# Normalised tokens stored as they are, the residual's gain and bias applied where the tokens return, in a two-layer diffusion backbone

## The chip, the cores and the metric

The kernel runs on one core of a Trainium2 chip. The time is device time of one execution in microseconds (us). Engines are called by the profile's names: PE is TensorE (PEld its weight loads), DVE VectorE, ACT ScalarE, POOL GpSimd, SP the engine on whose queue the kernel issues its DMAs. Each engine works through its own instructions in order.

## The reference

1024 latent tokens and 256 context tokens of width 1024, all fp32, pass two layers. Both layers end in a SwiGLU network of hidden width 2816. Layer 0 mixes with a gated convolution and a spatial gating unit, layer 1 with attention (8 heads, 2 key/value heads) over all tokens; the output is the latents'.

```python
def _post_norm(x, y, gate, g, b):
    return _layernorm(ALPHA * x + gate * y, g, b)

for l in range(DEPTH):
    m_lat = jnp.split((s_lat @ ada_w[l] + ada_b[l])[:, None, :], 6, axis=-1)
    m_ctx = jnp.split(s_ctx @ ada_w[l] + ada_b[l], 6, axis=-1)
    ...   # y_lat, y_ctx: convolution and gating unit (l = 0), or attention (l = 1)
    x = _post_norm(x, y_lat, m_lat[2], ln_g[l, 0], ln_b[l, 0])
    x = _post_norm(x, _swiglu(_modulate(x, m_lat[3], m_lat[4]), ffn_w_in[l], ffn_w_out[l]),
                   m_lat[5], ln_g[l, 1], ln_b[l, 1])
    ...   # the same for ctx in layer 0
```

So each normalised token is used twice: modulated, as input of the next product, and times ALPHA, as the residual of the next norm. With n the normalised token before gain and bias, the residual is n * (ALPHA * ln_g) + ALPHA * ln_b.

## The kernel before

The code is written against a tile framework whose scheduler orders the instructions of all engines by a simulated time line, within the dependences and the rings of buffers; it may move an instruction far ahead of or behind its place in the code. Rings are named by the tile: U (`u`), T (`tt`) and M2 (`m2`, shown as `m`) are general 128x512 buffers, T with few of them, and a weight pool has rings `raw`, `sw`, `w2`. An fp32 product is three products of split values (high x high, high x low, low x high; `mm3`, L88 to L90); `split` (L199 ACT copy, L200 DVE subtraction) makes the halves.

The order of work is: mixer for latents, then for context (0 to about 500 us); `ffn_in2` and `ffn_out2` for layer 0's latents (500 to 1185); the context's network, called from a hook in the last group of `ffn_out2` (to 1450); q, k, v (to 1600); attention (to 1905); the product with wo (to 2000); `ffn_in2` (2060 to 2450) and `ffn_out2` (to 2685) of layer 1; the last norm.

`ffn_in2` computes a pair of input products in seven products instead of eight: `ln_forms` transposes and modulates the normalised tokens to H and F (L483 to L493), `t_forms` makes four differences of them (L497) and splits them, and `weights(j)` makes seven weight forms for each of 22 column tiles. A tile uses the products in the order 1, 2, 6, 5, 7, 3, 4, where 6, 5, 7 and 4 take the forms t2, t1, t3 and t4. The first two products of the first `pre` tiles are made early. `ffn_out2` works in two halves of the hidden width (`kb`), for two halves of the columns (`h`) and two groups of four token tiles; DVE adds the residual `xr` to a sum (L646).

`ln_norm` normalises a tile: statistics on DVE, rs = (variance)^-0.5 on POOL (L212), the subtraction and product on DVE (L220). `resid` (L236 product, L239 sum, rows from `ln_row`, scaled on POOL at L227) then turns the normalised tile into the residual in place, 32 DVE steps for the latents' 16 half tiles, and `spill` stores it in DRAM. It is called after both latent mixers between `ln_forms` and `t_forms`; after `ffn_out2` of layer 0 it waits in `deferred`, which the context's network runs later.

`bg_ada` is a generator that makes the modulation vectors in the background: `step(n)` runs n of its pieces. A piece loads two blocks of ada_w and adds them up on DVE (L126, one step a block and vector); after four pieces POOL sums over partitions (`partition_all_reduce`, L132). (1, 1) and (1, 5) below are the layer and the index of such a vector.

Of the kernel before, what the change touches and what calls it, by code (L numbers as in the profile page):

```python
# [28 lines left out]
def hybrid_kernel(ctx: ExitStack, tc: tile.TileContext, A, out):  # L29
# [193 lines left out]
    def ln_row(nm, l, i, h, scale=True):  # L223
        t = M2([P, 512])
# [285 lines left out]
    def ffn_in2(pp, wq, l, H, act_d, steps=0, pre=2):  # L510
        def weights(j):
# [55 lines left out]
        for j in range(pre):  # L567
            p2(ready[j])
# [30 lines left out]
    def ffn_out2(pp, wq, l, act_d, xr, acc, steps=0, hook=None):  # L599
# [3 lines left out]
        for kb in range(2):  # L603
            aT = []
            for h in range(2):
                ws = []
                for k in range(KB):
# [13 lines left out]
                    hi = wq.tile([P, 512], F32R, tag="w2", name="w2", bufs=26)  # L621
                    lo = wq.tile([P, 512], F32R, tag="w2", name="w2", bufs=26)
                    split(w, hi, lo)
                    ws.append((hi, lo))
                for gi, grp in enumerate(grps):
# [3 lines left out]
                    pss = {}  # L629
# [8 lines left out]
                    def evict(t):  # L638
                        if kb == 0:
                            if h == 0:  # L640
                                acc[t] = [U([P, 512], F32), U([P, 512], F32)]
                            x = M2([P, 512])
                            nc.sync.dma_start(out=x, in_=xr[t * P:(t + 1) * P, h * 512:(h + 1) * 512])
# [9 lines left out]
                    else:  # L653
# [5 lines left out]
                        if kb == 1:  # L659
                            step(steps)  # L660

    def spill(xr):
        return lambda tiles, t0: (lambda t, h: nc.sync.dma_start(
            out=xr[(t0 + t) * P:(t0 + t + 1) * P, h * 512:(h + 1) * 512], in_=tiles[t][h]))
# [107 lines left out]
    for i in range(4):  # L772
        t_forms(H, F, i)
# [9 lines left out]
    def ctx_ffn_start():  # L783
# [8 lines left out]
        resid([accc[0], accc[1]], 0, 0, [nc.vector])  # L792
# [18 lines left out]
    xr_d = dp.tile([SEQ, D], F32, name="xr_d")  # L811
    hT = []
    for g in range(2):
        for t in range(4 * g, 4 * g + 4):
            ln_norm(acc[t])
        hT.append(ln_mod(pp, [acc[t] for t in range(4 * g, 4 * g + 4)], so))
    accl2 = [acc[t] for t in range(8)]
    deferred.append(lambda: resid(accl2, 0, 1, ENG, lambda t, h: nc.sync.dma_start(
        out=xr_d[t * P:(t + 1) * P, h * 512:(h + 1) * 512], in_=accl2[t][h])))
# [347 lines left out]
```

## Time and profile before

| | us |
|---|---|
| median of 3 runs | 2713.39 (2711.13 to 2713.71) |
| the profiled execution | 2716.35 |
| its span in the trace | 2714.6 |
| PE busy | 2548.0 (94%) |
| DVE busy | 1893.7 (70%) |
| ACT busy | 923.8 (34%) |
| POOL busy | 393.3 (14%) |
| mean granted PE clock | 0.972 of full speed |

Shares are of the whole span. What an engine does in a stretch, and what PE waits for there, is read from windows and from the idle time that the timeline gives in brackets before an instruction, with the engine and the instruction that ended it.

### The profile page before, as it was taken

How to read it: one execution, taken by the hardware profiler on the slowest of the kernel's cores; microseconds unless marked ns; L12 is line 12 of the kernel's file. 1: busy time of each engine (PE TensorE's matmuls, PEld its weight loads, DVE VectorE, ACT ScalarE, POOL GpSimd, SP SyncE). 2: the span in 40 equal slices, each digit the busy share in tenths (PEclk: the TensorE clock that was granted, in tenths of full speed). 3: DMA queues.
4: the chain of work that ended last, by engine and by line, in shares of the span. 5: the costliest groups of instructions: out<-in, count | busy, mean ns of one | idle time of the engine just before them, and what ended most of it. 6: DMA issues, size and time to landing. Idle time of an engine off the chain costs nothing. (4 is left out here: it accounts for less than half of the span.)

```text
span 2714.6 us, 34771 instructions
## 1 busy us (share of the span) xinstructions
PE 2548.0 (94%) x12956; PEld 2142.1 (79%) x12956; DVE 1893.7 (70%) x3203; ACT 923.8 (34%) x1628; POOL 393.3 (14%) x277
## 2 busy tenths in 40 slices
PE   8999986899999999967999999999978999999998
PEld 6778875787788887856997879999856888888886
DVE  3888497999966726767776767777599666665355
ACT  2311142433233412125443347777134333332121
POOL 0232031022200001230002432222030000000004
PEclk9999997999999999978999999999998999999999
DMA  7462144344422625535552200000412222235231
GB/s 248 137 199 86 57 132 161 132 152 137 124 92 72 221 78 184 182 118 171 187 177 95 106 13 1 25 24 24 147 55 105 93 72 91 77 120 181 85 105 62
DMA packets 152650, 307.39 MB, mean 113 GB/s; under 512 B 25312, under 2 KB 44768, under 8 KB 152480
## 3 DMA queue, kind: packets, MB, share of 16 engines
q1 hardware_dynamic: 152480, 305.16, 34.1%
q8 instruction: 102, 1.67, 0.2%
q14 instruction: 68, 0.56, 0.1%
HBM read 259.95 MB, written 45.15 MB: 112 GB/s over the span
## 5 line engine op out<-in xcount | busy, mean ns | idle before, releaser
L88 PE MATMUL mm<-u,w 128*128 128x512 f32 x1232 | 481.6, 393 | 30.5 <-ACT u L199 12.8
L90 PE MATMUL mm<-u,w 128*128 128x512 f32 x1232 | 476.1, 391 | 9.6 <-DVE w L200 9.6
L89 PE MATMUL mm<-u,w 128*128 128x512 f32 x1232 | 481.8, 391 | 1.7 <-DVE u L490 1.7
L199 ACT CAST w<-sw 128x512 fp32r<-128x512 f32 x264 | 163.1, 622 | 535.6 <-PE mm L89 397.4
L88 PEld LDWEIGHTS mm<-u,w 128*128 128x128 f32 x1232 | 232.6, 189 | 84.3 <-ACT u L199 13.7
L88 PE MATMUL mm<-w,u 128*128 128x512 f32 x704 | 275.1, 391 | 6.7 <-DVE u L646 4.6
L90 PEld LDWEIGHTS mm<-u,w 128*128 128x128 f32 x1232 | 232.5, 189 | 59.5 <-DVE w L200 11.0
L200 DVE TENSOR_TENSOR w<-sw,w 128x512 fp32r<-128x512 f32 x264 | 191.2, 727 | 125.8 <-ACT w L199 79.3
L89 PE MATMUL mm<-w,u 128*128 128x512 f32 x704 | 275.1, 391 | 0.0
L89 PEld LDWEIGHTS mm<-u,w 128*128 128x128 f32 x1232 | 232.7, 189 | 50.6 <-DVE u L490 2.7
L90 PE MATMUL mm<-w,u 128*128 128x512 f32 x704 | 269.6, 390 | 0.0
L88 PE MATMUL mm<-hi,u 128*128 128x512 f32 x664 | 257.4, 401 | 10.1 <-ACT hi L82 3.7
L89 PE MATMUL mm<-lo,u 128*128 128x512 f32 x664 | 262.1, 396 | 2.9 <-DVE lo L84 2.9
L82 ACT CAST hi<-wf 128x1024 fp32r<-128x1024 f32 x142 | 147.8, 1050 | 325.8 <-PE mm L90 91.9
L88 PE MATMUL mm<-u,hi 128*128 128x256 f32 (+1 forms) x736 | 239.8, 326 | 19.3 <-DVE u L292 11.6
L90 PE MATMUL mm<-hi,u 128*128 128x512 f32 x664 | 253.9, 394 | 0.0
L90 PE MATMUL mm<-u,lo 128*128 128x256 f32 (+1 forms) x736 | 238.8, 326 | 3.6 <-DVE lo L84 3.3
L89 PE MATMUL mm<-u,hi 128*128 128x256 f32 (+1 forms) x736 | 238.8, 324 | 0.0
L84 DVE TENSOR_TENSOR lo<-wf,hi 128x1024 fp32r<-128x1024 f32 x142 | 174.8, 1248 | 48.3 <-ACT hi L82 48.2
L212 POOL TENSOR_TENSOR rs<-ve,mhalf 128x1 f32<-128x1 f32 x36 | 30.8, 857 | 1129.4 <-DVE ve L210 1107.1
L88 PEld LDWEIGHTS mm<-u,hi 128*128 128x128 f32 x736 | 143.1, 194 | 32.0 <-DVE u L292 11.8
L88 PEld LDWEIGHTS mm<-w,u 128*128 128x128 f32 x704 | 132.7, 188 | 35.5 <-DVE u L646 5.0
(172 smaller groups left out, 4778.3 us busy)
## 6 DMA issues: line engine op xcount, KB each, us to landing
raw<-in_ffn_in SPq DMA_DIRECT2D x88, 512.0 KB
act<-m SPq DMA_DIRECT2D x88, 256.0 KB
raw<-act SPq DMA_DIRECT2D x44, 512.0 KB
sw<-in_ffn_out SPq DMA_DIRECT2D x88, 256.0 KB
wf<-in_ffn_in SPq DMA_DIRECT2D x44, 512.0 KB
wf<-in_w_m SPq DMA_DIRECT2D x32, 512.0 KB
m<-in_ada_w SPq DMA_DIRECT2D x64, 256.0 KB
ab<-in_ada_w SPq DMA_DIRECT2D x48, 256.0 KB
```

The costliest lines, as they stand in the source:

```text
L82: nc.scalar.copy(hi, wf)
L84: (lo_eng or nc.vector).tensor_tensor(out=lo, in0=wf, in1=hi.bitcast(F32), op=ALU.subtract)
L88: nc.tensor.matmul(ps, s[0], m[0], start=first, stop=False, skip_group_check=more)
L89: nc.tensor.matmul(ps, s[0], m[1], start=False, stop=False, skip_group_check=more)
L90: return nc.tensor.matmul(ps, s[1], m[0], start=False, stop=last, skip_group_check=more)
L199: nc.scalar.copy(hi, src)
L200: return nc.vector.tensor_tensor(out=lo, in0=src, in1=hi.bitcast(F32), op=ALU.subtract)
L212: marks["pow"] = nc.gpsimd.tensor_tensor(out=rs, in0=ve, in1=mhalf[:, 0:1], op=ALU.pow)
```

## The change

`resid` is no longer called for latents. `ln_spill` stores the normalised tile, and gain and bias are applied where it comes back: in `ffn_out2` ahead of a group's products (`xs`, L645 and L646 of the new code), and for the attention's residual in `resid_bg`, which the attention loop calls 16 times to turn `xn2_d` into `xr_d`. The sums of `bg_ada` move: eight pieces at two places of the first half of `ffn_out2` instead of 14 at two of the second, and those of (1, 5) into `ffn_in2` of layer 1. `t_forms` makes and splits the forms in the order of use; three tiles are begun early instead of two; the product with wo takes its weights from the pool that `ffn_in2` uses next (22 instead of 26 buffers `w2`).

```diff
-    def t_forms(H, F, i):
-        f11, f21, f12, f22 = F[0, 0, i], F[1, 0, i], F[0, 1, i], F[1, 1, i]
-        sub(f11, f12, f11)
-        sub(f12, f22, f12)
-        sub(f22, f22, f11)
-        sub(f21, f21, f22)
-        for n, f in ((1, f11), (2, f22), (3, f12), (4, f21)):
+    def t_forms(H, F):
+        def form(n, f):
             hi, lo = U([P, 512], F32R), U([P, 512], F32R)
             split(f, hi, lo)
             H.setdefault(("t", n), []).append((hi, lo))
 
-    def ffn_in2(pp, wq, l, H, act_d, steps=0, pre=2):
+        for i in range(4):
+            f11, f12, f22 = F[0, 0, i], F[0, 1, i], F[1, 1, i]
+            sub(f11, f12, f11)
+            sub(f12, f22, f12)
+            sub(f22, f22, f11)
+            form(2, f22)
+        for i in range(4):
+            form(1, F[0, 0, i])
+        for i in range(4):
+            form(3, F[0, 1, i])
+        for i in range(4):
+            sub(F[1, 0, i], F[1, 0, i], F[1, 1, i])
+            form(4, F[1, 0, i])
+
+    def ffn_in2(pp, wq, l, H, act_d, steps=0, pre=3):
...
+                if kb == 0:
+                    rg, rb = ln_row("ln_g", l, 0, h, buf=T), ln_row("ln_b", l, 0, h, buf=T)
...
-                    pss = {}
+                    pss, xs = {}, {}
+                    if kb == 0:
+                        for t in grp:
+                            xs[t] = M2([P, 512])
+                            nc.sync.dma_start(out=xs[t], in_=xn[t * P:(t + 1) * P, h * 512:(h + 1) * 512])
+                            nc.vector.tensor_tensor(out=xs[t], in0=xs[t], in1=rg, op=ALU.mult)
+                            nc.vector.tensor_tensor(out=xs[t], in0=xs[t], in1=rb, op=ALU.add)
...
-                        if kb == 1:
+                        if kb + h == 1:
                             step(steps)
...
+    def ln_spill(a, t, xn):
+        ln_norm(a)
+        for h in range(2):
+            nc.sync.dma_start(out=xn[t * P:(t + 1) * P, h * 512:(h + 1) * 512], in_=a[h])
...
-    for a in tiles[0]:
-        ln_norm(a)
-    ln_forms(pp, tiles[0], so, 0, H, F)
-    for a in tiles[1]:
-        ln_norm(a)
-    resid(tiles[0], 0, 0, ENG, spill(xr0_d)(tiles[0], 0))
-    ln_forms(pp, tiles[1], so, 1, H, F)
-    resid(tiles[1], 0, 0, ENG, spill(xr0_d)(tiles[1], 4))
+    for g in range(2):
+        for t, a in enumerate(tiles[g]):
+            ln_spill(a, 4 * g + t, xr0_d)
+        ln_forms(pp, tiles[g], so, g, H, F)
...
-    ada_buf.update(aw=singles(lambda: M2([P, 512])), ac=singles(T), rd=singles(T), ahead=2, end=1000)
-    ffn_out2(pp, wq, 0, act_d[0], xr0_d, acc, steps=14, hook=ctx_ffn_start)
-    need(1, 5)
+    ada_buf.update(ac=singles(T), rd=singles(T), end=72)
+    ffn_out2(pp, wq, 0, act_d[0], xr0_d, acc, steps=8, hook=ctx_ffn_start)
...
+    def resid_bg(n):
+        t, h = divmod(n, 2)
+        x = T()
+        nc.sync.dma_start(out=x, in_=xn2_d[t * P:(t + 1) * P, h * 512:(h + 1) * 512])
+        nc.vector.tensor_tensor(out=x, in0=x, in1=rows[h][0], op=ALU.mult)
+        nc.vector.tensor_tensor(out=x, in0=x, in1=rows[h][1], op=ALU.add)
+        nc.sync.dma_start(out=xr_d[t * P:(t + 1) * P, h * 512:(h + 1) * 512], in_=x)
...
+        if b % 9 == 8 and b // 9 < 16:
+            resid_bg(b // 9)
...
+    ada_buf.update(ac=UF, rd=UF, end=80)
+    ffn_in2(pp, wq, 1, H, act_d[1], steps=1)
```

What the scheduler makes of it is seen in the order of each engine's queue.

On DVE, between layer 0's forms and the context mixer (`L490` and `L497` make forms, `L80` and `L84` prepare the mixer's weights), there stands before:

```order
L236 TENSOR_TENSOR u_1489<-u_1489,m2_3100 128x512
L236 TENSOR_TENSOR u_1523<-u_1523,m2_3100 128x512
L236 TENSOR_TENSOR u_1557<-u_1557,m2_3100 128x512
L236 TENSOR_TENSOR u_1591<-u_1591,m2_3100 128x512
L497 TENSOR_TENSOR u_2887<-u_3047,u_2887 128x512
L497 TENSOR_TENSOR u_2898<-u_3054,u_2898 128x512
L84 TENSOR_TENSOR lo_3454<-wf_3449,hi_3452 128x1024
```

In the changed program the queue at the same place, down to the gating unit's norm (`L328` to `L335`), reads:

```order
L328 BN_STATS st1_3131<-u_3129 128x6
L497 TENSOR_TENSOR u_3063<-u_3063,u_2895 128x512
L328 BN_STATS st1_3167<-u_3165 128x6
L497 TENSOR_TENSOR u_3074<-u_3074,u_2906 128x512
L330 BN_AGGR mv_3133<-st1_3131 128x2
L497 TENSOR_TENSOR u_2939<-u_2939,u_3063 128x512
L330 BN_AGGR mv_3169<-st1_3167 128x2
L497 TENSOR_TENSOR u_2950<-u_2950,u_3074 128x512
L332 TENSOR_SCALAR ve_3135<-mv_3133 128x1
L332 TENSOR_SCALAR ve_3171<-mv_3169 128x1
L335 TENSOR_SCALAR u_3129<-u_3129,mv_3133,rs_3137 128x512
```

All 32 steps of L236 and L239 have gone from this stretch; L328 moved to just ahead of L335, and the rest is the same work.

On DVE at the end of the k and v tiles and the start of the attention, where before the queue goes from the last tile's steps to the split of the transposed keys, the changed program has (L1055 and L1056 are `resid_bg`, `tr_13121` and `tr_13122` the transposed keys, `pt` the scores):

```order
L1055 TENSOR_TENSOR tt_13662<-tt_13662,m2_13319 128x512
L880 TENSOR_TENSOR tt_13290<-tt_13290,rs4_13288 128x256
L1055 TENSOR_TENSOR tt_13895<-tt_13895,m2_13325 128x512
L1056 TENSOR_TENSOR tt_13662<-tt_13662,m2_13322 128x512
L1055 TENSOR_TENSOR tt_14133<-tt_14133,m2_13319 128x512
L1056 TENSOR_TENSOR tt_13895<-tt_13895,m2_13328 128x512
L1055 TENSOR_TENSOR tt_14369<-tt_14369,m2_13325 128x512
L200 TENSOR_TENSOR u_13304<-tr_13121,u_13303 128x512
L200 TENSOR_TENSOR u_13308<-tr_13122,u_13307 128x512
L1056 TENSOR_TENSOR tt_14133<-tt_14133,m2_13322 128x512
```

All 32 steps stand within 56 rows; the last of them is followed by the first split of the probabilities (`ph`).

On POOL, in `ffn_out2` and around the norm after it, an `ISA` row without names stands wherever the kind of operation changes (L132 the all-reduce, L212 rs, L227 the rows of gain and bias). Before, the stretch around the norm is:

```order
L212 TENSOR_TENSOR rs_9774<-ve_9772,mhalf_80 128x1
L227 TENSOR_SCALAR m2_9460<-m2_9460 128x512
L227 TENSOR_SCALAR m2_9463<-m2_9463 128x512
L227 TENSOR_SCALAR m2_9470<-m2_9470 128x512
L132 ISA
L132 ISA tt_9375<-tt_9352 128x512
L212 ISA
L212 TENSOR_TENSOR rs_9785<-ve_9783,mhalf_80 128x1
```

In the changed program the last rows ahead of the norm are:

```order
L227 ISA
L227 TENSOR_SCALAR m2_9962<-m2_9962 128x512
L132 ISA
L132 ISA tt_9060<-tt_8893 128x512
L115 MEMSET tt_9063 128x512
L227 ISA
L227 TENSOR_SCALAR m2_9965<-m2_9965 128x512
L227 TENSOR_SCALAR m2_9972<-m2_9972 128x512
L227 TENSOR_SCALAR m2_9975<-m2_9975 128x512
L132 ISA
L132 ISA tt_9086<-tt_9063 128x512
L212 ISA
```

All all-reduces stand ahead of the first rs now, and the stretch from the start of `ffn_out2` has seven such rows without names in place of three.

## Rows read from the trace of the kernel before

**Rows 1.** The page: busy tenths of PE in 40 equal slices of the span

```profile
PE   8999986899999999967999999999978999999998
```

**Rows 2.** Windows: length, busy us of PE PEld DVE ACT POOL, clock, DMA share, GB/s

```profile
400.00:430.00 30.00, 1.73 (x12) 1.15 (x14) 29.48 (x50) 6.36 (x10) 18.71 (x3) 0.53 0.54 193
1183.00:1215.00 32.00, 7.00 (x30) 4.67 (x29) 14.15 (x30) 7.47 (x13) 7.75 (x9) 0.61 0.25 86
1183.00:1285.00 102.00, 57.93 (x366) 52.26 (x365) 69.57 (x108) 44.50 (x66) 13.24 (x10) 0.75 0.42 142
2000.00:2050.00 50.00, 23.16 (x100) 15.87 (x99) 48.18 (x82) 29.00 (x47) 21.53 (x4) 0.73 0.34 121
```

**Rows 3.** Timeline of PE at A: start, us, instruction, idle before it and releaser

```profile
404.67 0.69 PE L351 MATMUL tr<-m,ones 128*64 128x128 f32 x4 [3.52 <-ACT u L326]
429.62 0.69 PE L361 MATMUL tr<-m,u 128*64 128x128 f32 x4 [24.26 <-DVE u L335]
```

**Rows 4.** Timeline of DVE at A

```profile
415.42 1.27 DVE L328 BATCH_NORM_STATS2 st<-u 128x6 f32<-128x512 f32 x2
...
428.93 1.16 DVE L335 TENSOR_SCALAR u<-u,mv,rs 128x512 f32<-128x512 f32 x2 [0.45 <-POOL rs L334]
```

**Rows 5.** Timeline of PE at C

```profile
1193.19 0.69 PE L258 MATMUL tr<-ident,u 128*128 128x128 f32 x2 [6.59 <-ACT tt L193]
...
1206.04 1.11 PE L258 MATMUL tr<-ident,u 128*128 128x128 f32 x4 [10.58 <-ACT tt L193]
...
1278.31 0.58 PE L88 MATMUL mm<-u,hi 128*128 128x256 f32 x1 [11.56 <-DVE u L292]
```

**Rows 6.** Timeline of POOL at C and just before it

```profile
1166.47 1.21 POOL L212 TENSOR_TENSOR rs<-ve,mhalf 128x1 f32<-128x1 f32 x2 [8.13 <-issue]
...
1189.30 3.25 POOL L132 PARTITION_ALL_REDUCE tt<-tt  x1 [6.05 <-issue]
1200.01 0.59 POOL L212 TENSOR_TENSOR rs<-ve,mhalf 128x1 f32<-128x1 f32 x1 [7.47 <-issue]
```

**Rows 7.** Timeline of SP's queue at C

```profile
1206.39 1.38 SPq L78 DMA_DIRECT2D wf<-in_ffn_in  x3
```

**Rows 8.** Timeline of DVE at C

```profile
1200.64 1.71 DVE L220 TENSOR_SCALAR u<-u,mv,rs 128x512 f32<-128x512 f32 x2 [15.36 <-POOL rs L212]
...
1258.84 8.51 DVE L236 TENSOR_TENSOR u<-u,m 128x512 f32<-128x512 f32 x14
1267.27 8.51 DVE L239 TENSOR_TENSOR u<-u,m 128x512 f32<-128x512 f32 x14
```

**Rows 9.** B: PE's longest wait on the timeline, and DVE's group of L239 (2000 to 2065)

```profile
2039.00 1.32 PE L88 MATMUL mm<-u,w 128*128 128x512 f32 x2 [12.78 <-ACT u L199]
...
L239 DVE TENSOR_TENSOR u<-u,m 128x512 f32<-128x512 f32 x16 | 10.8, 680 | 0.0
```

**Rows 10.** Timeline of DVE at the start of the attention: key split, first probability split

```profile
1601.87 1.29 DVE L200 TENSOR_TENSOR u<-tr,u 128x512 fp32r<-128x512 f32 x2 [1.04 <-ACT u L199]
...
1614.36 1.27 DVE L200 TENSOR_TENSOR u<-tr,ph 128x512 fp32r<-128x512 f32 x2
```

**Rows 11.** Windows around the attention's start, and of three other stretches

```profile
1575.00:1600.00 25.00, 22.77 (x106) 18.46 (x104) 11.91 (x46) 4.73 (x12) 9.16 (x12) 1.00 0.03 11
...
1625.00:1650.00 25.00, 25.00 (x185) 23.54 (x183) 19.48 (x43) 18.56 (x45) 6.72 (x5) 1.00 0.01 2
0.00:25.00 25.00, 18.80 (x134) 13.11 (x135) 7.58 (x15) 6.50 (x7) 0.69 (x6) 1.00 0.98 312
...
950.00:975.00 25.00, 25.00 (x112) 20.71 (x111) 4.50 (x7) 1.87 (x3) 0.00 (x0) 1.00 0.24 74
...
2075.00:2100.00 25.00, 25.00 (x112) 20.71 (x111) 19.40 (x33) 8.37 (x14) 0.00 (x0) 1.00 0.33 121
```

**Rows 12.** Seam of ffn_out2, from the timeline of PE; the sums of ada_w, from the line's view

```profile
1062.27 0.80 PE L88 MATMUL mm<-w,u 128*128 128x512 f32 x1 [4.58 <-DVE u L646]
...
L126 DVE SCALAR_TENSOR_TENSOR u<-u,sc x96: 736/744/2729, 516.8 to 724.9; 128x512 f32<-128x512 f32 x96
```

More of the change, by code (lines that the diff above doesn't have):

```diff
@@ L567, in ffn_in2 @@
         for j in range(pre):
-            p2(ready[j])
+            p2(ready[j], lambda: U([P, 512], F32))
         for j in range(NJ):
@@ L597, in ffn_in2, with ffn_out2 @@
             step(steps if j % 2 else 0)
-    def ffn_out2(pp, wq, l, act_d, xr, acc, steps=0, hook=None):
+    def ffn_out2(pp, wq, l, act_d, xn, acc, steps=0, hook=None):
         gate = gate_bc(0, l, 5)
@@ L771, in hybrid_kernel @@
     mixer(pp, hc, 1, A["cx"], accc)
-    for i in range(4):
-        t_forms(H, F, i)
+    t_forms(H, F)
     xn_d = dp.tile([CTX, D], F32, name="xn_d")
@@ L791, in ctx_ffn_start @@
         hcf.append(ln_mod(pp, [accc[0], accc[1]], so))
-        resid([accc[0], accc[1]], 0, 0, [nc.vector])
+        deferred.append(lambda: resid([accc[0], accc[1]], 0, 0, [nc.vector]))
     wpA.__exit__(None, None, None)
@@ L797, in hybrid_kernel, with AD @@
     wq = wpF.__enter__()
+    def AD():
+        return wq.tile([P, 512], F32, tag="ad", name="ad", bufs=4)
     UF = singles(lambda: U([P, 512], F32))
-    ada_buf.update(aw=UF, ac=UF, rd=UF, ahead=1, end=48)
+    ada_buf.update(aw=singles(AD), ac=UF, rd=UF, ahead=2, end=48)
     ffn_in2(pp, wq, 0, H, act_d[0], steps=3)
@@ L811, in hybrid_kernel @@
     xr_d = dp.tile([SEQ, D], F32, name="xr_d")
+    xn2_d = dp.tile([SEQ, D], F32, name="xn2_d")
     hT = []
@@ L814, in hybrid_kernel @@
         for t in range(4 * g, 4 * g + 4):
-            ln_norm(acc[t])
+            ln_spill(acc[t], t, xn2_d)
         hT.append(ln_mod(pp, [acc[t] for t in range(4 * g, 4 * g + 4)], so))
-    accl2 = [acc[t] for t in range(8)]
-    deferred.append(lambda: resid(accl2, 0, 1, ENG, lambda t, h: nc.sync.dma_start(
-        out=xr_d[t * P:(t + 1) * P, h * 512:(h + 1) * 512], in_=accl2[t][h])))
     hc = hcf
@@ L1034, in score_piece @@
             score_c(n, 1)
+    rows = [[ln_row(nm, 0, 1, h) for nm in ("ln_g", "ln_b")] for h in range(2)]
+    def resid_bg(n):
[5 more added lines that the diff above has]
+        nc.sync.dma_start(out=xr_d[t * P:(t + 1) * P, h * 512:(h + 1) * 512], in_=x)
     for n in range(LOOK):
@@ L1051, in hybrid_kernel, with prep_wo @@
     pp = ppC.__enter__()
-    wpC = tc.tile_pool(name="wpC", bufs=4, reuse_waits="tile")
-    wp = wpC.__enter__()
+    wpD = tc.tile_pool(name="wpD", bufs=3, reuse_waits="tile")
+    wq = wpD.__enter__()
     gate = gate_bc(0, 1, 2)
+    def prep_wo(k):
+        raw = wq.tile([P, 1024], F32, tag="raw", name="raw", bufs=3)
+        nc.sync.dma_start(out=raw, in_=A["wo"][k])
+        nc.vector.tensor_tensor(out=raw, in0=raw, in1=gate, op=ALU.mult)
+        w = []
+        for h in range(2):
+            hi = wq.tile([P, 512], F32R, tag="w2", name="w2", bufs=22)
+            lo = wq.tile([P, 512], F32R, tag="w2", name="w2", bufs=22)
+            split(raw[:, h * 512:(h + 1) * 512], hi, lo)
+            w.append((hi, lo))
+        return w
     acc = {}
     for kv in range(2):
-        ws = [prep(A["wo"][kv * 4 + h], gate) for h in range(4)]
+        ws = [prep_wo(kv * 4 + h) for h in range(4)]
         for t in range(8):
@@ L1064, in hybrid_kernel @@
                 for k in range(4):
[L1065 removed]
+                    mm3(ps, a[k], ws[k][h], k == 0, k == 3)
                 if kv == 0:
@@ L1075, in hybrid_kernel @@
     tiles = [[acc[t] for t in range(4 * g, 4 * g + 4)] for g in range(2)]
-    for a in tiles[0]:
-        ln_norm(a)
-    ln_forms(pp, tiles[0], so, 0, H, F)
-    for a in tiles[1]:
-        ln_norm(a)
-    resid(tiles[0], 1, 0, ENG, spill(xr1_d)(tiles[0], 0))
-    ln_forms(pp, tiles[1], so, 1, H, F)
-    for i in range(4):
-        if i == 2:
-            resid(tiles[1], 1, 0, ENG, spill(xr1_d)(tiles[1], 4))
-        t_forms(H, F, i)
-    wpC.__exit__(None, None, None)
-    wpD = tc.tile_pool(name="wpD", bufs=3, reuse_waits="tile")
-    wq = wpD.__enter__()
+    for g in range(2):
+        for t, a in enumerate(tiles[g]):
+            ln_spill(a, 4 * g + t, xr1_d)
+        ln_forms(pp, tiles[g], so, g, H, F)
+    t_forms(H, F)
     acc = {}
-    ffn_in2(pp, wq, 1, H, act_d[1])
+    ada_buf.update(ac=UF, rd=UF, end=80)
+    ffn_in2(pp, wq, 1, H, act_d[1], steps=1)
     ffn_out2(pp, wq, 1, act_d[1], xr1_d, acc)
```

23 lines of the change are left out of this document (9 added, 14 removed).

## The prediction

> **What bounds the kernel now.** I read the page first: TensorE (PE) is busy in nearly every slice, and the few slices at 6 and 7 tenths are where time can be won [rows 1]. The windows say what happens there. In 400 to 430 us PE works 1.73 us of 30 while VectorE (DVE) works 29.48; in 1183 to 1285 PE works 57.93 of 102; in 2000 to 2050 23.16 of 50, with DVE at 48.18. The granted clock there means 0.53, 0.75 and 0.73, so part of the work ran at the lower of the two levels, 1.2 GHz; in the dense products it is 1.00, 2.4 GHz, and 112 full products take 25 us, 0.223 us each [rows 2, 11]. I call the three places A, C and B. They hold about 28 + 44 + 27 = 99 us of idle PE (the spans less the busy time).
>
> The rows of each place give the wait that ends last. **A**: PE stands 24.26 us for u of L335 [rows 3]. Among what stands ahead of L335 in its queue are the 32 steps of `resid` (L236, L239): a run of fourteen such steps takes 8.51 us [rows 8], 0.605 a step, and at A they stand between runs of other work without a gap, down to L328 at 415.42 and L335 at 428.93 [rows 4]. **C** has two halves. First, PE stands 6.59 and 10.58 us for modulated transposes [rows 5]; behind them DVE's L220 stands 15.36 us for rs, and POOL shows why: an all-reduce stands between two runs of rs, with 6.05 us in front of it, 7.47 after it and 8.13 before the first rs, in which POOL waits for nothing shown [rows 6]. I read these as changes of POOL's program. The SP queue stands behind the same things: the first context weights are asked for at 1206.39 [rows 7]. Second, PE stands 11.56 us for L292, which stands in DVE's queue behind 28 steps of `resid` in one piece from 1258.84, 17 us [rows 5, 8]. **B**: PE stands 12.78 us for a split form, with 32 more steps of `resid` (its 16 of L239 take 10.8 us) in DVE's queue [rows 9].
>
> **The change, part by part.** Sums are made against the profiled execution's own 2716.35 us, which is 3.0 above the median 2713.39.
>
> *A.* Exactly the 32 steps leave the queue ahead of L335; what is left there is the same work. 32 x 0.605 = 19.4 us of a queue without gaps. L328's input is ready only at about 404.7, where PE's earlier wait ends [rows 3], and in the new order some 6 us of DVE work stand between L328 and L335, so L335 cannot come before about 411, against 428.93: 18 us, from 15 (ScalarE or the transposes late) to 22 (some half-clock work goes too). I take **-18**.
>
> *C, first half.* The 16 sums of (1,1) and (1,5) that lay around the norms go into ffn_out2's first half and into ffn_in2 of layer 1; the last change of POOL's program now comes before the first rs, and the context weights no longer queue behind the all-reduce. PE's idle here is 32 - 7.00 = 25.0 us [rows 2]; the norm's chain (statistics, rs, L220, modulation, transposes) still has to run, and I keep 3 to 8 us of waits for it: 17 to 22 gained. *Second half:* the latents' 32 steps leave; L292 needs PE's sums, not them, and its 11.56 us of wait go [rows 5]. Between the halves PE had a mean clock of 0.75 over 102 us and 57.93 us of busy time, of which at most 58 x 0.25 = 14.5 was lost to the clock; I give back 3 to 12. Together 28 to 48; I take **-38**.
>
> *B.* 32 steps leave (19.4 us), the splits of weight pairs 0 and 1 move ahead of the last output sums, the form used first is made first, and a third early pair adds 24 products (24 x 0.223 = 5.4 us) with which PE bridges DVE. From the last output sum to the first wait for a DVE result of the forms' product the queue has 54 rows in place of 102. 27 us of idle PE and at most 23.16 x 0.27 = 6 us of lost clock [rows 2] are there to win; PE's shorter waits for transposes stay. 18 to 31; I take **-25**.
>
> *What comes back: the residual in attention.* The code spreads 16 loads, 32 DVE steps and 16 stores over the attention, but the order has all 32 in one burst at its start: the first stands before the last key tile's L880, seven stand ahead of the split of the transposed keys, and the last stands just before the first split of the probabilities. At that place before, the key split is done at about 1603 and the first split of probabilities starts at 1614.36 [rows 10], and PE idles 2.2 us in 1575 to 1600 and none in 1625 to 1650, where DVE works 19.5 of 25 and DMA moves almost nothing [rows 11]. The burst costs DVE 19.4 us and moves 32 x 0.262 MB = 8.39 MB through five buffers; at 312 GB/s, the fastest window of the trace [rows 11], that is 26.9 us. The Trainium skill's page "DMA: Bandwidth & Descriptors", Specifications, sets a limit of about 358 GB/s for one core's HBM share; by it the transfers alone would be 23.4 us, and the trace at a share of 0.98 does not reach it. PE's cover is 36 score products (8 to 12 us). If the loads start at about 1598, the first split of probabilities comes near 1626 and PE loses 12 to 15 us. From below it is 0: DVE has 13 idle us in 1575 to 1600, and the loads can go as soon as buffers come free. From above: each of three rounds of the ring takes load, two steps and store in series, and if load and store move one after the other at half that rate the 26.9 become 54, of which the 13 idle us of DVE and the cover of 8 to 12 hide some 20: 35. I take **+14**. Attention cannot give it back, PE being full there.
>
> *POOL and DVE in ffn_out2, layer 0.* 32 multiply and add steps (19.4 us) join DVE, spread over the first four groups; a group is 132 products, 29.5 us, and DVE worked 4.5 us of 25 at 950 to 975 [rows 11], so they are covered. But POOL gets seven program changes there in place of three, because rows of ln_g and ln_b now alternate with reduces. At 6 to 8 us each that is 42 to 57 us, most of it under products. The Trainium skill's page "GPSIMD Engine Reference", Instruction dispatch, gives about 6 us for the first call of a newly loaded kernel; by it the seven are 42 us, and the rows, 6.05 to 8.13, agree or lie higher. What counts is who stands behind: DVE's column step (L175) and an SP transfer wait for the last reduce, and the weights of the second half stand behind them. Before, PE lost 4.6 us at this seam [rows 12]; now between 2 and 23. Change: -3 to +18, taken **+4**, since a group's 29.5 us of products mostly covers a chain of two changes.
>
> *Sums in ffn_in2, layer 1.* 16 sums at 0.744 us [rows 12] are 11.9 us of DVE among products that bound it (25.0 of 25 by PE, DVE 19.4, at 2075 [rows 11]); three reduces on POOL. 0 to +11; **+2**. In ffn_in2 of layer 0 the sums' number is the same: 0.
>
> Sum: -18 - 38 - 25 + 14 + 4 + 2 = -61: 2655 from this execution, 2652 from the median. I say **2653**.
>
> **Rivals.** (1) *The burst hides.* DVE's idle time before 1600 takes it, and POOL's changes fall under products: the two positive terms go to about 2, and the time is 2638. For it: DVE at 11.91 of 25 in 1575 to 1600. Against: the buffers of the ring are the same that the key tiles use. (2) *The wins are half of it*, because DVE or ScalarE, not `resid`, ends the waits at C and B once `resid` is gone (chains of rs, modulation and splits with other steps late next): C -22, B -14, A -15, with +20 of costs: 2717 - 31 - 3 = 2683. For it: ScalarE works 44.5 of 102 us at C and is itself named as the releaser. (3) *Slower*: the seam in ffn_out2 stalls. If SP and DVE wait for a reduce that waits for several changes in series, PE stops until the seven changes are through; 57 us, less the 29.5 of one group, are 27, and the burst at its upper end 35: 62 of cost meets 81 of gain. It decides only if the stall at the seam passes about 46 us, that is if weights for more than one group come late. (4) *The change does not do what it says*: the scheduler could have kept the work where it was; the order excludes that for A, C and B, and shows it for the attention.
>
> **How the numbers follow.** Forecast 0.50, rival 1 0.22, rival 2 0.22, rival 3 0.04, rival 4 0.02. A difference below 0.2% is about what a measurement of this kernel cannot tell from none. Faster 0.94, same 0.02, slower 0.04. The forecast's bounds are -18 +/- 4, -38 +/- 10, -25 +/- 6, +14 +/- 14, +4 +/- 10, which as independent errors give about 20; the range takes in rivals 1 and 2: 2622 to 2688.
>
> **What would show it.** A: PE's wait for L335 under 9 us. C: no step of `resid` for latents between 1180 and 1290, no L220 waiting over 8 us for rs, and PE busy over 80% there. B: PE's wait for the forms' split under 5 us. Attention: L1055 and L1056 in one block, PE idle some 14 us for the first splits. Seam: PE's wait at the second half of ffn_out2 under 12 us. I am wrong if PE at C still waits over 20 us, or if the seam costs over 20.

## The result, and the profile after

The changed kernel takes 2667.29 us (median of 4 runs, 2663.14 to 2670.20) against 2712.84 before (4 runs): a ratio of 0.9832, 95% interval 0.9815 to 0.9849, so 45.6 us are gained where 60 were forecast. The span of its profiled execution is 2668.4 us, 46.2 less.

To see where they came from I cut both executions at the same seven instructions. The view of a line or a tile gives the first and the last start of a group; these are the rows of before (the last two numbers ahead of the semicolon are the starts):

```profile
L361 PE MATMUL tr<-m,u x160: 272/273/476, 89.2 to 441.5; 128*64 128x128 f32 x160
L646 DVE TENSOR_TENSOR u<-m,mm x32: 673/685/689, 963.7 to 2583.0; 128x512 f32<-128x512 f32 x32
L646 DVE TENSOR_TENSOR u<-u,mm x32: 635/679/689, 1097.4 to 2704.3; 128x512 f32<-128x512 f32 x32
L292 DVE TENSOR_TENSOR u<-u,mm x84: 633/680/689, 227.8 to 1442.1; 128x512 f32<-128x512 f32 x84
L88 PE MATMUL sa<-u x128: 387/396/500, 1601.5 to 1889.2; 128*128 128x512 f32 x128
L1071 DVE TENSOR_TENSOR u<-u,mm x16: 630/680/689, 1967.9 to 1999.4; 128x512 f32<-128x512 f32 x16
L550 DVE TENSOR_TENSOR m<-m,mm x88: 673/681/689, 530.0 to 2472.0; 128x512 f32<-128x512 f32 x88
```

And the same groups after the change, by their new line numbers:

```profile
L361 PE MATMUL tr<-m,u x160: 272/273/476, 88.9 to 422.8; 128*64 128x128 f32 x160
L662 DVE TENSOR_TENSOR u<-m,mm x32: 677/682/689, 946.8 to 2536.8; 128x512 f32<-128x512 f32 x32
L662 DVE TENSOR_TENSOR u<-u,mm x32: 669/678/689, 1087.1 to 2658.1; 128x512 f32<-128x512 f32 x32
L292 DVE TENSOR_TENSOR u<-u,mm x84: 632/679/689, 227.9 to 1392.0; 128x512 f32<-128x512 f32 x84
L88 PE MATMUL sa<-u x128: 388/396/797, 1551.9 to 1865.6; 128*128 128x512 f32 x128
L1109 DVE TENSOR_TENSOR u<-u,mm x16: 632/681/689, 1937.5 to 1980.4; 128x512 f32<-128x512 f32 x16
L559 DVE TENSOR_TENSOR m<-m,mm x88: 669/679/689, 514.8 to 2426.4; 128x512 f32<-128x512 f32 x88
```

The differences of neighbouring starts are the lengths of the stages:

| stage | before | after | difference | forecast |
|---|---|---|---|---|
| to the last gating transposes (A): last L361 | 441.5 | 422.8 | -18.7 | -18 |
| ffn_in2, layer 0: to the first u<-m sum | 522.2 | 524.0 | +1.8 | 0 |
| the seam: to the first u<-u sum | 133.7 | 140.3 | +6.6 | +4 |
| rest of ffn_out2, norm, context network (C): to the last L292 | 344.7 | 304.9 | -39.8 | -38 |
| q, k, v: to the first score | 159.4 | 159.9 | +0.5 | 0 |
| attention: to the last score's first product | 287.7 | 313.7 | +26.0 | +14 |
| end of attention, product with wo: to its last sum | 110.2 | 114.8 | +4.6 | 0 |
| forms and ffn_in2, layer 1 (B): to the last m<-m sum | 472.6 | 446.0 | -26.6 | -25 + 2 |
| ffn_out2, layer 1: to its last sum | 232.3 | 231.7 | -0.6 | 0 |
| sum | 2704.3 | 2658.1 | -46.2 | -61 |

The windows of [rows 2] look like this after the change (length, busy us of PE, PEld, DVE, ACT, POOL, granted clock, DMA share, GB/s); the last one is new, the start of the attention:

```profile
1183.00:1285.00 102.00, 96.69 (x684) 92.10 (x685) 79.02 (x100) 57.69 (x80) 4.79 (x4) 0.95 0.52 170
400.00:430.00 30.00, 20.24 (x114) 15.25 (x114) 22.31 (x43) 8.90 (x16) 1.17 (x2) 0.73 0.21 70
2000.00:2050.00 50.00, 45.93 (x189) 35.75 (x188) 49.39 (x79) 25.87 (x44) 4.42 (x3) 0.93 0.33 104
1550.00:1600.00 50.00, 32.23 (x157) 26.21 (x158) 43.32 (x83) 21.68 (x49) 9.84 (x8) 0.76 0.55 180
```

Most of each of the three holes is filled, though the stages have moved by 10 to 50 us under these windows. A new one has opened, where before PE idled little [rows 11]. PE's timeline there:

```profile
1567.79 0.80 PE L88 MATMUL sa<-u 128*128 128x512 f32 x1 [8.44 <-ACT pt L990]
...
1577.26 0.47 PE L1005 MATMUL tr<-ident,pt 128*128 128x128 f32 x1 [2.89 <-POOL pt L999]
```

PE waits for the exponential of the first scores (L990). DVE's timeline says why that is late: the steps of the softmax (L985 to L988) stand between those of `resid_bg` (L1055, L1056), some of which wait for their loads.

```profile
1560.93 0.69 DVE L1055 TENSOR_TENSOR tt<-tt,m 128x512 f32<-128x512 f32 x1 [0.58 <-DMA tt<-xn_d]
1561.54 0.68 DVE L1056 TENSOR_TENSOR tt<-tt,m 128x512 f32<-128x512 f32 x1
1562.14 1.22 DVE L986 TENSOR_REDUCE mx<-sa 128x1 f32<-128x1024 f32 x1
1563.28 0.68 DVE L1056 TENSOR_TENSOR tt<-tt,m 128x512 f32<-128x512 f32 x1
1563.88 0.41 DVE L985 TENSOR_REDUCE mx<-pt 128x1 f32<-128x256 f32 x1
1564.56 0.69 DVE L1055 TENSOR_TENSOR tt<-tt,m 128x512 f32<-128x512 f32 x1 [0.27 <-DMA tt<-xn_d]
```

Windows over the whole stage split its loss in two (the attention before, then after, then 15 us of it after the change):

```profile
1601.50:1889.20 287.70, 283.82 (x2033) 262.89 (x2032) 224.70 (x491) 208.57 (x491) 82.34 (x62) 1.00 0.06 18
1551.90:1865.60 313.70, 292.97 (x2033) 268.01 (x2032) 243.47 (x516) 208.40 (x490) 82.12 (x61) 0.96 0.14 44
1565.00:1580.00 15.00, 7.96 (x19) 5.29 (x20) 12.39 (x24) 5.34 (x13) 2.42 (x2) 0.50 0.61 204
```

With the same number of products (2033), PE idles 20.73 us (the length less the busy time) in place of 3.88, 16.85 more. The products themselves take 9.15 us longer: between PE's waits the granted clock is 0.50, the lower of its two levels.

### The profile page after: what moved, and what is told of

Read it like the earlier page. It is cut to its first block, busy times and chain, and to the rows that moved or that the text cites. A ratio compares the mean times of both kernels' runs of the same rounds, so it can differ in the third digit from the quotient of the medians.

```text
span 2668.4 us, 34907 instructions
## 1 busy us (share of the span) xinstructions
PE 2553.8 (96%) x12956; PEld 2143.0 (80%) x12956; DVE 1895.5 (71%) x3211; ACT 925.4 (35%) x1636; POOL 347.9 (13%) x269
## 4 chain that ended last, share of the span: by engine, by line
PE 75%; DVE 10%; DMA 4%; ACT 3%; issue 3%; POOL 1%; SPq 0%; DVEq 0%; ACTq 0%; POOLq 0%
PE mm L88 22%; PE mm L89 22%; PE mm L90 22%; PE tr L1005 2%; DMA wf<-in_ffn_out 1%; PE tr L89 1%; PE tr L90 1%; PE tr L88 1%; DVE u L200 1%; DVE lo L84 1%; DVE u L126 1%; DVE w L200 1%; PE sa L90 1%; PE sa L88 1%; PE sa L89 1%
## 5 line engine op out<-in xcount | busy, mean ns | idle before, releaser
L88 PE MATMUL mm<-u,w 128*128 128x512 f32 x1232 | 480.8, 393 | 11.6 <-DVE m L559 5.9
L88 PE MATMUL mm<-w,u 128*128 128x512 f32 x832 | 326.1, 395 | 12.2 <-ACT u L199 5.9
L89 PE MATMUL mm<-w,u 128*128 128x512 f32 x832 | 326.3, 393 | 0.0
L90 PE MATMUL mm<-w,u 128*128 128x512 f32 x832 | 320.5, 391 | 2.6 <-DVE u L200 2.6
L200 DVE TENSOR_TENSOR w<-sw,w 128x512 fp32r<-128x512 f32 x264 | 186.3, 708 | 79.4 <-ACT w L199 53.0
L82 ACT CAST hi<-wf 128x1024 fp32r<-128x1024 f32 x134 | 139.5, 1051 | 273.3 <-PE mm L90 92.2
L88 PE MATMUL mm<-hi,u 128*128 128x512 f32 x536 | 208.4, 400 | 7.3 <-DVE tt L875 3.1
L89 PE MATMUL mm<-lo,u 128*128 128x512 f32 x536 | 210.8, 395 | 3.2 <-DVE lo L84 3.2
L90 PE MATMUL mm<-hi,u 128*128 128x512 f32 x536 | 203.7, 395 | 0.0
L88 PEld LDWEIGHTS mm<-w,u 128*128 128x128 f32 x832 | 158.1, 190 | 48.0 <-ACT u L199 7.2
L84 DVE TENSOR_TENSOR lo<-wf,hi 128x1024 fp32r<-128x1024 f32 x134 | 164.4, 1246 | 37.5 <-ACT hi L82 37.1
L90 PEld LDWEIGHTS mm<-w,u 128*128 128x128 f32 x832 | 157.1, 189 | 36.3 <-DVE u L200 3.7
L89 PEld LDWEIGHTS mm<-w,u 128*128 128x128 f32 x832 | 157.9, 190 | 32.6
```

The lines of the kernel that those rows point to most:

```text
L82: nc.scalar.copy(hi, wf)
L84: (lo_eng or nc.vector).tensor_tensor(out=lo, in0=wf, in1=hi.bitcast(F32), op=ALU.subtract)
L88: nc.tensor.matmul(ps, s[0], m[0], start=first, stop=False, skip_group_check=more)
L89: nc.tensor.matmul(ps, s[0], m[1], start=False, stop=False, skip_group_check=more)
L90: return nc.tensor.matmul(ps, s[1], m[0], start=False, stop=last, skip_group_check=more)
L200: return nc.vector.tensor_tensor(out=lo, in0=src, in1=hi.bitcast(F32), op=ALU.subtract)
```

## The experiments

Each kernel is the changed one with the edit shown. Ratios are to the kernel before, with their 95% intervals; the changed kernel's is 0.9832 (0.9815 to 0.9849). Stage lengths are cut as in the table above.

**e1_spread: the same steps, kept apart.** One dependence is added in `resid_bg`:

```diff
-        nc.sync.dma_start(out=x, in_=xn2_d[t * P:(t + 1) * P, h * 512:(h + 1) * 512])
+        i1 = nc.sync.dma_start(out=x, in_=xn2_d[t * P:(t + 1) * P, h * 512:(h + 1) * 512])
+        after(i1, [norm[-1]])
```

> The changed kernel (2667 us) with one dependence more: the load of each resid_bg is ordered behind the last softmax normalisation written before it, so that its two VectorE steps stand one or two units apart along the attention and not in a burst at its start. From the first score to the last, the attention took 314.2 us after the change and 288.2 before, 26 more. Theory 1 (the place costs: VectorE steps stand in a burst ahead of the first softmax steps): 20 to 24 us come back, 2643 to 2648 us. Rival (the work costs wherever it stands, since TensorE is full and VectorE works 20 of 25 us in the attention): under 8 us come back, 2660 or more, with TensorE's waits spread along the attention.

Measured: 2662.47 us, ratio 0.9809 (0.9796 to 0.9822). The attention takes 305.7 us, 8.0 less than with the burst, and 18.0 more than before. Theory 1 falls: the place is worth 8 us of the 26. PE's waits over the attention, by instruction and releaser (us, times, longest):

```profile
PE tr L88 <- DMA u<-q_d: 5.5, 4, 2.4
PE tr L89 <- DVE u L200: 4.8, 12, 0.4
PE sa L88 <- ACT pt L990: 3.2, 6, 1.2
```

The long wait is gone, and short ones for DVE's splits stand all along the attention. The first row is a wait that was not there: the loads of q for the later tiles land late. They share SP's queue with the 32 transfers, some of which wait for DVE; that this holds them is argued, not tried. So the 18.0 us over the time before are not owed to the steps alone.

**e2_moves: the transfers without the steps.** The two `nc.vector.tensor_tensor` lines of `resid_bg` are taken out.

> The changed kernel with the 32 VectorE steps of resid_bg left out; its 16 loads and 16 stores stay (the attention's residual is then without gain and bias). Theory 1a (VectorE's steps are the cost): the wait of TensorE at the attention's start falls by 15 us or more, 2652 us or less. Theory 1b (the transfers through five buffers are the cost, VectorE only waits for them): 2660 or more. VectorE stood 4.9 us for these loads in the trace after the change, so I expect 2649, and 2645 if the waits for loads go too.

Measured: 2650.40 us, 0.9766 (0.9753 to 0.9779); the attention takes 292.9 us. **e3_none: neither.**

```diff
...
-        if b % 9 == 8 and b // 9 < 16:
-            resid_bg(b // 9)
...
-                    nc.sync.dma_start(out=xr, in_=xr_d[t * P:(t + 1) * P, h * 512:(h + 1) * 512])
+                    nc.sync.dma_start(out=xr, in_=xn2_d[t * P:(t + 1) * P, h * 512:(h + 1) * 512])
```

> The changed kernel without resid_bg: no loads, steps or stores, the product with wo adds the stored normalised tokens (the attention's residual is left without gain and bias). It bounds what resid_bg costs in all. Theory 1: 26 us, 2641. If the attention's loss came from something else in the change (order of the key tiles, buffers), it stays above 2655.

Measured: 2646.35 us, 0.9745 (0.9732 to 0.9759); the attention takes 293.5 us. So `resid_bg` costs 313.7 - 293.5 = 20.2 us of the attention, and the transfers alone cost nothing there (292.9). Theory 1a holds against 1b: the cost belongs to the 32 steps, 19.4 us of DVE. That it is so near to their length does not mean that PE stands for each of them. Without `resid_bg` the stage is

```profile
1550.10:1843.60 293.50, 287.69 (x2032) 265.20 (x2032) 224.32 (x486) 208.27 (x489) 81.97 (x61) 0.99 0.06 17
```

PE idles 5.81 us in it. So the burst costs 14.9 us of idle time (20.73 - 5.81), and 5.3 us (292.97 - 287.69) by which the products take longer. Spread along the attention, `resid_bg` costs 12.2 us (305.7 - 293.5), 5.5 of which are the waits for q. And 5.8 us (293.5 - 287.7) of the attention's loss have nothing to do with `resid_bg`: the kernels without it took from 291.0 to 293.6 us. What is known of these stands below under the hardware.

**e4_wo: gain and bias where the product with wo adds the residual.**

```diff
-        if b % 9 == 8 and b // 9 < 16:
-            resid_bg(b // 9)
...
-                    xr = M2([P, 512])
-                    nc.sync.dma_start(out=xr, in_=xr_d[t * P:(t + 1) * P, h * 512:(h + 1) * 512])
+                    xr = T()
+                    nc.sync.dma_start(out=xr, in_=xn2_d[t * P:(t + 1) * P, h * 512:(h + 1) * 512])
+                    nc.vector.tensor_tensor(out=xr, in0=xr, in1=rows[h][0], op=ALU.mult)
+                    nc.vector.tensor_tensor(out=xr, in0=xr, in1=rows[h][1], op=ALU.add)
```

> The changed kernel with gain and bias applied in the product with wo, where the tokens return, as ffn_out2 does it: no resid_bg, no second store and load. The order shows 10 of the 32 steps still at the attention's start (five buffers are free for early loads), 22 in the product with wo, where VectorE works 10 to 20 of 25 us. Theory 1: the start costs 10 x 0.6 = 6 us instead of 21, and the product with wo at most 3 more: 2651 to 2656. Rival (the product with wo cannot take them, its sums wait): 2662 or more.

Measured: 2643.96 us, 0.9740 (0.9727 to 0.9754), as good as leaving the residual's gain and bias out. The attention takes 291.2 us (scores from 1548.4 to 1839.6), and from there to wo's last sum it is 115.5, 0.7 more than after the change. The first of these windows is of the product with wo in e4_wo, the second lies at about the same place of the stage in the changed kernel, which has no such steps there:

```profile
1850.00:1900.00 50.00, 47.24 (x227) 39.73 (x227) 42.40 (x63) 10.34 (x19) 0.00 (x0) 0.93 0.44 153
1875.00:1925.00 50.00, 47.23 (x238) 40.04 (x237) 29.86 (x42) 11.06 (x20) 0.11 (x1) 0.97 0.46 153
```

DVE has 42.40 of 50 us to do in place of 29.86, a little more than its share in the attention [rows 11], but PE works as long as without the steps. I read it so that what PE multiplies is ready before, and only sums wait; no run tests this reading. Even the ten steps that stand at the attention's start cost nothing that can be seen. My expectation of 6 us for them was too high.

**e5_rows: the rows scaled on VectorE.** In `ln_row` the product takes an argument for its engine, and `ffn_out2` and the context's `resid` pass `nc.vector`.

```diff
-            nc.gpsimd.tensor_scalar(out=t, in0=t, scalar1=ALPHA, scalar2=1.0, op0=ALU.mult, op1=ALU.mult)
+            (eng or nc.gpsimd).tensor_scalar(out=t, in0=t, scalar1=ALPHA, scalar2=1.0, op0=ALU.mult, op1=ALU.mult)
```

> The changed kernel with the rows of gain and bias in ffn_out2 and in the context's residual scaled on VectorE instead of GpSimd, so that only all-reduces and then rs stand in GpSimd's queue there (one change of program in place of seven). After the change the seam of ffn_out2 of layer 0 cost 6.6 us more than before (first sum of the first half to first sum of the second: 140.3 us against 133.7), and its last all-reduce came 8.5 us after the work before it. Theory (GpSimd's changes hold that all-reduce, SP's queue stands behind it and the second half's activations are asked for late): 6 us come back, 2661. Rival (the added VectorE steps or the buffers of the rows hold the weights): under 2 us, 2665 or more.

Measured: 2663.09 us, 0.9817 (0.9804 to 0.9831), whose interval overlaps with that of the changed kernel. The stage tells more than the total: the seam takes 134.4 us in place of 140.3. It takes from 133.7 to 134.4 in the four kernels with this edit, and from 137.1 to 140.4 in the changed kernel and those that leave the seam as it is there (e6_ada, below, does not); between the means, 134.1 and 139.1, lie 5.0 us. After the change, POOL's last all-reduces there and the load behind them were:

```profile
1029.89 3.51 POOL L132 PARTITION_ALL_REDUCE tt<-tt  x1 [7.34 <-issue]
...
1049.46 1.07 POOL L227 TENSOR_SCALAR m<-m 128x512 f32<-128x512 f32 x1 [15.57 <-DVE w L200]
...
1053.53 0.83 POOL L227 TENSOR_SCALAR m<-m 128x512 f32<-128x512 f32 x1 [0.78 <-DMA m<-in_ln_b]
1062.85 3.25 POOL L132 PARTITION_ALL_REDUCE tt<-tt  x1 [8.49 <-DVE u L200]
```

```profile
1066.13 0.24 SPq L135 DMA_DIRECT2D mrow<-tt  x1
1066.47 0.32 SPq L622 DMA_DIRECT2D raw<-act  x1
```

The profile puts the last gap down to a split (L200), but the last of the sums that this all-reduce adds up was done at 1051.06; in e5_rows, where no rows stand ahead of it, it starts at 1051.88, right behind DVE's last sum. So a good part of the seam's cost is owed to the rows that stand between the all-reduces in GpSimd's queue, with SP's queue behind them. That the gaps of 7.34 and 8.49 us are changes of GpSimd's program is how I read them.

**e6_ada: the sums of ada_w as before the change.** The lines of `ffn_out2`'s call, of its `step` and of layer 1's `ffn_in2` are put back (`steps=14`, `if kb == 1:`, `need(1, 5)`).

> The changed kernel with the sums of ada_w as before the change: 14 pieces at two places of the second half of ffn_out2, the rest before the norm, none in ffn_in2 of layer 1. The stage from the seam to the context network's last sum became 39.8 us shorter by the change. Theory (its first half is owed to the moved sums and their all-reduces, its second to the residual's steps): 17 to 22 us are lost again, less what the seam and ffn_in2 of layer 1 give back: 2680 to 2690. Rival (all of it is owed to the residual's steps): 2672 or less.

Measured: 2675.55 us, 0.9868 (0.9853 to 0.9884). It tells little of what it was made for: with this kernel's buffers the scheduler put all all-reduces ahead of the first rs, the last at 1103.22, so stage C stayed short (301.7 us), and the seam took 148.1. By the code the changed kernel's `step` runs at four places, two in each half of `ffn_out2`, and at three of the second half in this run and before; but the scheduler placed them otherwise. After the change all 48 sums of these places start between 936.1 and 1050.0, ahead of the second half's first sum, and here they do so too, with the 16 of (1,5) behind them, to 1102.3. What follows is only that the seam is 8 us longer with these 16 there.

**e9_norm: all-reduces among the rs.** The sums of (1,5) are held back until the norm:

```diff
...
+        if g == 0:
+            marks["hold"] = marks["pow"]
+            ada_buf.update(end=80)
+            need(1, 5)
+            del marks["hold"]
...
```

These loads of ada_w are ordered behind `marks["hold"]`, the pool of the weights is closed behind this place, and layer 1's `ffn_in2` runs without sums.

> The changed kernel with the 16 sums of (1,5) and their two all-reduces held back until the first four rs of the norm after ffn_out2; in GpSimd's queue an all-reduce then stands between the seventh and the eighth rs, as one stood between the fifth and the sixth before the change. e6_ada had moved no all-reduce between the rs, so it could not tell. Theory (such an all-reduce, with GpSimd's changes of program on both sides, holds L220 and the transposes behind it, and SP's queue holds the context's weights): the stage from the second half's first sum to the context network's last sum, 304.9 us after the change, grows by 12 to 22 us; 2680 to 2690 in all. Rival (that stage's whole gain is owed to the residual's steps): under 5 us, 2672 or less.

Measured: 2689.91 us, 0.9929 (0.9907 to 0.9950). Stage C takes 327.9 us (1083.4 to 1411.3), 23.0 more. POOL's timeline has the pattern of [rows 6] again:

```profile
1178.71 3.25 POOL L134 PARTITION_ALL_REDUCE tt<-tt  x1 [9.66 <-DMA ad<-in_ada_w]
...
1189.37 0.59 POOL L214 TENSOR_TENSOR rs<-ve,mhalf 128x1 f32<-128x1 f32 x1 [6.92 <-issue]
1199.08 3.51 POOL L134 PARTITION_ALL_REDUCE tt<-tt  x1 [9.12 <-issue]
```

and PE stands for it, most of all for the context's first weights:

```profile
1182.83 1.12 PE L260 MATMUL tr<-ident,u 128*128 128x128 f32 x4 [5.76 <-ACT tt L195]
...
1202.12 0.58 PE L88 MATMUL mm<-u,hi 128*128 128x256 f32 x1 [16.83 <-ACT hi L82]
```

Before the change these weights cost PE 5.92 us and the transposes 22.6; here it is 16.83 and 7.5. In SP's queue the loads of ada_w stand right ahead of the weights:

```profile
1191.69 2.69 SPq L101 DMA_DIRECT2D ad<-in_ada_w  x4
1194.43 1.37 SPq L78 DMA_DIRECT2D wf<-in_ffn_in  x3
```

After the change the weights are asked for at 1174.30. So the 23.0 us are the price of the whole work on (1,5) at this place, its loads and the later closing of the pool included, and not of the all-reduces alone.

**e10_defer: the latents' residual back in the context network.** `ln_spill` becomes `ln_norm` for these tiles, `resid_bg` goes, and the deferred call of before is put back.

> The changed kernel with the latents' residual of layer 0's end applied in place where it was before the change (the deferred 32 steps inside the context's network, stored as xr_d); resid_bg is gone. Theory (those steps cost 11 to 18 us where they stand in one piece ahead of the context's sums, and the attention gives back what e3_none gave, 21): 2667 + 15 - 21 = 2661, from 2657 to 2664. Rival (they cost nothing there, because the gain of that stage is owed to the moved sums): 2646 to 2650.

Measured: 2667.74 us, 0.9842 (0.9824 to 0.9859), no different from the changed kernel. Stage C takes 327.6 us (1081.5 to 1409.1), 22.7 more, and the attention 293.6, 20.1 less. PE idles 27.58 us in C in place of 10.39 and its products take 300.02 us in place of 294.51. Its longest waits:

```profile
PE mm L88 <- DVE u L292: 9.1, 1, 9.1
PE mm L89 <- DVE lo L84: 6.9, 2, 5.8
```

The wait for L292 is that of [rows 5] come back. The theory holds, with 23 us where I had put 15.

**e7_forms: the old order of the forms, two early tiles.** `t_forms` makes and splits the four forms tile by tile again, and `pre=2`.

> The changed kernel with the forms made in the old order and two early tiles instead of three. The stage from the last sum of the product with wo to the last product of ffn_in2 became 26.6 us shorter. Theory (the 32 residual steps that left are some 19 of it, order and third tile some 6): 2671 to 2676. Rival (order and early tile are more than half of it): 2680 or more.

Measured: 2664.64 us, 0.9822 (0.9806 to 0.9837): no difference in all, where 2671 to 2676 was expected. Stage B takes 450.9 us, 4.9 more, near the 6 of the expectation, but layer 0 gives it back: its `ffn_in2` takes 516.9 us in place of 524.0.

**e8_both** joins e4_wo and e5_rows.

> Gain and bias applied in the product with wo (as in e4_wo, 2644 us) and the rows scaled on VectorE (as in e5_rows). If the seam's 6.6 us are owed to GpSimd's changes and the two effects are independent: 2638 us; if the rows have no effect: 2644.

Measured: 2641.82 us, 0.9739 (0.9726 to 0.9752); the seam takes 133.7 us (943.4 to 1077.1). In the total e5's edit cannot be told from nothing here.

**e11_best and e12_pre** put layer 0 back on e8_both's base: e12_pre by the number of early tiles alone, e11_best with the old order of the forms as well:

```diff
-    ffn_in2(pp, wq, 0, H, act_d[0], steps=3)
+    ffn_in2(pp, wq, 0, H, act_d[0], steps=3, pre=2)
```

> e8_both (2642 us) with the old order of forms and two early tiles in layer 0 alone. In e7_forms layer 0's stage from the last gating transposes to the first sum of ffn_out2 was 7 us shorter than after the change (516.9 against 524.0 us), layer 1's stage 4.9 longer. If both hold alone: 2635 us. If the two layers' stages hang together through the buffers: 2640 or more.

> e8_both with two early tiles in layer 0 and the new order of forms in both layers. Theory (the third early tile's splits stand in VectorE's queue ahead of what TensorE waits for in layer 0, where the sums of ada_w keep VectorE full): 2635, like e11_best. Rival (the order of the forms is the cause): 2642, like e8_both.

Measured: 2629.56 us, 0.9698 (0.9681 to 0.9715), and 2632.07 us, 0.9705 (0.9688 to 0.9721). Both beat e8_both beyond the intervals and cannot be told from each other: the third early tile costs layer 0 its 7 us, and the order of the forms nothing clear of the noise. PE's waits from 430 to 760 us, in e8_both and then in e12_pre:

```profile
PE mm L90 <- DVE w L200: 7.5, 2, 5.3
PE mm L88 <- DVE m L559: 5.8, 7, 2.3
```

```profile
PE mm L90 <- DVE w L200: 4.8, 1, 4.8
PE mm L88 <- DVE m L559: 4.1, 5, 1.7
```

With three tiles PE waits a second time for a split weight (w), early in `ffn_in2`, and longer for the sums. e11_best is the fastest kernel: 0.9698 of the kernel before.

## Why the prediction was right, and where it was off

**A, C and B** came as the sum had them: -18.7, -39.8 and -26.6 where -18, -38 and -25 (with +2) stood.

At A, PE's wait for L335 ends at 411.35, where the sum had about 411. A was not tried alone.

For C both of its causes were put back by themselves. The 32 steps ahead of L292 cost 22.7 us (e10_defer); the work on (1,5) among the rs cost 23.0 (e9_norm), though mostly by another wait than before the change. Together they are more than the 39.8 that the stage gained, so the shares cannot be added; I had split it into 17 to 22, 11.6 and 3 to 12 for the clock (together 32 to 46, not the 28 to 48 of the sum), and that the total came within 2 us is in part luck. The sums that lay around the norms were those of (1,5) alone: those of (1,1) were done by 725 us [rows 12].

For B, e7_forms gives 4.9 us to the order and the third tile, 5.4 in the sum. It leaves 21.7 to the rest, the residual's steps and the earlier weight splits, which no run takes apart; some 3 of these are work of the stage that only moved ahead of the cut (below). The sums in layer 1's `ffn_in2` show no cost: without them stage B took 450.9 us in e6_ada and 448.1 in e9_norm, not less.

Of the marks that I had set, PE's wait for L335 was 9.52 us, a little over the 9; PE's busy share at C is 95% (over 80 was asked), its waits for a split form at B are under 2 us, and those in the window of the seam sum to 11.0. At the attention's start PE idles 17.8 us in 1550 to 1600, where some 14 were asked.

**The term that was mis-sized is the attention's: +26.0 where +14 was taken.** The burst stood where the order showed it. Of the 26.0, 16.85 are idle time of PE, not far from the 14. The other 9.15 are products at the lower clock, which this term put at nothing, though those of C and B counted it. And the idle time came near by luck, for its reason was wrong: I took the burst's length from the transfers, 26.9 us at 312 GB/s. With all transfers and without the steps nothing is lost (e2_moves), so the resource is DVE. The burst also took longer: from the first load, issued at 1545.29, to the first split of the probabilities at 1586.79 it is 41.5 us. That split comes 34.9 us behind the first score in place of 12.9, 22.0 later where the sum had 12. The steps share DVE's queue with what the score products need: a score bank comes free only after DVE's maximum and ScalarE's exponential, and the maximum stood behind the steps, as it must where the last step is just ahead of that split. So the cover that I had counted on (8 to 12 us of score products, 13 idle us of DVE ahead of 1600) hid little. The first step starts at 1550.19, 1.7 us ahead of the first score; I read that so that the buffers came free only with the last key tiles. Rival 1, the hidden burst, falls with it. 5.8 of the 26.0 do not come from `resid_bg` at all (e3_none).

**The seam** (+6.6 for +4) was right in mechanism: some 5 us of it go when the rows leave GpSimd's queue (e5_rows and the kernels built on it).

**What I had at nothing:** the third early tile costs layer 0 some 7 us (e7_forms, e12_pre), hidden in the table because the stage changed by +1.8 in all; what gave the other 5 there was not tried. (One candidate is a part of the change that the section on it does not name: the loads of ada_w have a ring of their own, `ad`, in place of U and M2.) The 4.6 us between the last score and wo's last sum were not foreseen, but most of them are no loss: 14 transposes (L483) and 2 products of the next stage stand ahead of this cut after the change, 2.6 us of work, which B has less, and 1.1 of waits.

**Rival 2** (2683) lies 16 us above the measured time, the forecast 14 below; but no half of C or B was lost, as it had it. Only the costs went its way: they came to 39 us (26.0, 6.6, 4.6 and 1.8; some 35 without the work that only moved across a cut), where it had 20 and the sum of the forecast 20 as well.

## What to carry to other kernels

Work that leaves the queue of an engine that others wait for is worth about its full time, and put elsewhere on that queue where the waits are tight it costs as much again: 32 steps of 0.605 us cost 20 to 23 us in the attention and in the context's product, 15 to 17 of them as TensorE's idle time and 5 as products at the lower clock. They cost nothing that can be seen in the product with wo, where VectorE was as busy but, as I read it, TensorE's next operands did not come from it. So look for the stage whose products do not wait for the engine, not for the one in which it idles most on average. Count the clock with a wait that you add as well as with one that you take away. A helper placed along a loop by hand does not stay there under a scheduler that may hoist it; read the order that came out. And cut the time at fixed instructions into stages: a change of many parts that gains 46 us hid a loss of 7 us in one layer from an edit that gained 5 in the other.

## What the runs showed of the hardware

The same wait was followed by two clocks. Before the change PE stood 3.11 us at the start of the attention and the granted clock stayed 1.00; in e3_none it stood 3.11 us at the same place, and the clock was then 0.50, the lower level, for 5 us (the wait and windows of 5 us, of before and then of e3_none):

```profile
1600.88 0.44 PE L926 MATMUL tr<-ident,tt 128*128 128x128 f32 x2 [3.11 <-DVE tt L867]
...
1600.00:1605.00 5.00, 4.11 (x21) 3.23 (x22) 3.83 (x8) 2.59 (x5) 0.37 (x1) 1.00 0.00 0
```

```profile
1548.96 0.69 PE L939 MATMUL tr<-ident,tt 128*128 128x128 f32 x2 [3.11 <-DVE tt L880]
...
1550.00:1555.00 5.00, 5.00 (x16) 4.03 (x15) 3.29 (x6) 2.28 (x5) 0.00 (x0) 0.50 0.00 0
1555.00:1560.00 5.00, 3.66 (x18) 2.68 (x17) 3.92 (x9) 4.33 (x12) 1.33 (x1) 0.99 0.02 3
```

In e1_spread it stood 3.11 us there too, and the clock stayed 1.00. What PE did in the 10 us before was alike in kind, so I cannot say from these rows what decides it. 5 us of products at half the clock are 2.5 us lost. Of the 5.8 us that the attention lost without `resid_bg`, 3.87 are longer products (287.69 against 283.82) and 1.93 idle time; what else made these stays open.

GpSimd's scaling of a row (L227) takes from 0.8 to 1.1 us in the timeline of e5_rows' section; before the change, beside VectorE's run of steps at A, one of them took 18.56 us, most of POOL's 18.71 busy us in 400 to 430 [rows 2], while the two rows ahead of it took 0.62 and 0.90. Why was not tried.
